# The context half of one attention block's first layer, run before and beside the experts of the block ahead of it

## The chip, the cores and the metric

One core of a Trainium2 chip runs the whole kernel. The metric is the device time of one execution in microseconds (us), the median of three runs.

## What is computed

Two blocks of two layers each work on 256 tokens of width 1024. Block 1 has a mixer and a mixture of 16 experts per layer; block 2 has attention and an MLP, on the tokens and, in layer 0, on 256 context tokens as well. All of it is float32.

```python
def first_block(x, c, ...):
    for layer in range(2):
        sh1, sc1, g1, sh2, sc2, g2 = split(silu(c) @ mod_w[layer] + mod_b[layer], 6)
        x = x + g1 * (even_mixer if layer == 0 else odd_mixer)(rms_norm(x) * (1 + sc1) + sh1)
        x = x + g2 * moe(rms_norm(x) * (1 + sc2) + sh2)      # 2 of 16 experts per token
    return x

def second_block(x, c, ctx, c_ctx, ...):
    xc = ctx
    for l in range(2):
        ...                                   # six modulation vectors for x, six for xc
        y, yc = _token_mixers(h, hc, ..., with_ctx_out=l == 0)
        x = _layer_norm(ALPHA * x + g1 * y)
        x = _layer_norm(ALPHA * x + g2 * _sq_relu_mlp(x * (1 + sc2) + sh2, w_fc1[l], w_fc2[l]))
        if l == 0:
            xc = _layer_norm(ALPHA * xc + g1c * yc)
            xc = _layer_norm(ALPHA * xc + g2c * _sq_relu_mlp(xc * (1 + sc2c) + sh2c, w_fc1[l], w_fc2[l]))
    return x
```

In `_token_mixers` the queries of the tokens see the keys of the tokens and of the context; the queries of the context see the context's keys alone. So nothing in the context half of layer 0 needs block 1.

## The kernel before

Activations stand transposed: `xT` and `cT` hold 8 tiles of 128 channels by 256 tokens, for the tokens and the context. A weight matrix is read in strips of 1024 x 128 (512 KB, one load on SP's queue, L321). `split_w` (L333, L325) makes of a strip a rounded part `wh` on ACT and a rest `wl` on VectorE, and `linear` (L345 to L347) multiplies in three matmuls per 128 channels, 24 for a strip; the moving operand is 256 columns wide for one half, 512 for both.

The phases follow each other: `ev` (layer 0's mixer), `moe0`, `od` (layer 1's mixer), `moe1`, then for each layer of block 2 `at` (attention) and `ml` (output, norm, MLP).

In a `moe` phase a router (L664 on) ranks the experts by the number of their tokens; `values_load` (L870) reads the 16 expert numbers into registers of SP. `PASSES` lists seven passes of one, one, two, two, two, four and four experts, which share the 128 columns of the array; `prep` gathers the tokens of the passes of a group in `GROUPS`, `up_` multiplies by w1 and w3, `down` by w2, `combine` adds the result to `xT`. Each expert has 12 loads of 512 KB, 192 in a phase, used as they are, in float32 (L917). While `deep` is set, loads go to 11 buffers named `raw` and to the 8 split buffers `wh` and `wl`.

In layer 0 of block 2 both halves go through each stage together: projections 512 columns wide (`lin`), `attend` for the tokens over 512 keys and for the context over 256, `out2`, and `mlp2` with 64 strips, of which 16 are read and multiplied once for each half.

The modulation vectors are 24 groups of eight steps (`mod_steps`, L365 on): a step loads 512 KB and multiplies it by the condition in small matmuls on PE (L396), or, where `onv` says so, by operations on VectorE (L388). They wait in `queue`; `fill(n)` issues the next n wherever it stands, `need` those up to a named group.

The instructions of each engine stand in an order that is fixed when the kernel is built, planned from the order of the program and the waits; each engine takes its own in that order.

Of the kernel before, what the change touches and what calls it, by code (L numbers as in the profile page):

```python
# [19 lines left out]
S = 256  # L20
# [3 lines left out]
GROUPS = [[0, 1], [2, 3], [4, 5, 6]]  # L24
# [177 lines left out]
def body(tc, A, out, co, po):  # L202
# [4 lines left out]
    with ExitStack() as ctx:  # L207
# [19 lines left out]
        def U(dt=F32, name="u", bufs=1, pool=None):  # L227
            return (pool or pools[-1][0]).tile([128, 512], dt, tag=name, bufs=bufs, name=name)

        def K1(name, bufs=2, pool=None):  # L230
            return (pool or pools[-1][0]).tile([128, S], F32, tag=name, bufs=bufs, name=name)

        class Act:


            def __init__(self, n, w=S, dt=F32, name="a", bufs=None, pool=None):
                self.w, self.per = w, 512 // w
# [65 lines left out]

        turn, more, XR, XH = [0, -1, -1], [], 5, 1

        deep = [None]

        def load(src, sh=None, w=1024):
            turn[1] += 1
            if deep[0]:  # L310
                pool, tag, n = deep[0][turn[1] % len(deep[0])]
                t = pool.tile([128, 1024], F32 if tag == "raw" else F32R, tag=tag, bufs=n, name=tag)
                t = t if tag == "raw" else t.bitcast(F32)
                d = SY.dma_start(out=t[:, :w] if sh is None else t[:, :w].rearrange("p (a b) -> p a b", a=sh), in_=src)
                return t, d.ins.name
# [5 lines left out]
            SY.dma_start(out=dst, in_=src)  # L321
# [119 lines left out]
        def colsum(src, nk, w=S):  # L441
# [10 lines left out]
            e = U(name="cs", bufs=2)  # L452
# [5 lines left out]
        def rstd_of(dst, o, n, ep=0):  # L458
# [5 lines left out]
            t = U(name="nr", bufs=2)[:, :w]  # L464
# [189 lines left out]
        landed = mybir.DependencyInfo(mybir.DependencyClass.Sync, mybir.DependencyReason.DATA)  # L654
# [14 lines left out]
        def router(xg, rs, sh):  # L669
# [26 lines left out]
            def rank(v, n):  # L696

                t = pools[-1][0].tile([128, n, 2, 4], F32, tag=f"rk{n}", bufs=2, name="rk")
# [34 lines left out]
            big = lambda: pools[-1][0].tile([128, 2, 16, 16], F32, tag="pm", bufs=2, name="pm")  # L733
# [44 lines left out]
        def wide3(n):  # L778
            sh = {"P": [128, 2, 384], "PT": [128, 3, S], "xg": [128, 8, 384]}[n]
            return pools[-1][0].tile(sh, F32 if n == "xg" else F32R, tag=n, bufs=2, name=n)  # L780
# [65 lines left out]
        def moe(l):  # L846
# [733 lines left out]
```

## Time and profile before

| | us |
|---|---|
| median of 3 runs (lowest, highest) | 1975.26 (1973.67, 1975.89) |
| the profiled execution | 1974.64 |
| its span, from the first to the last instruction | 1972.9 |
| busy: PE, VectorE (DVE), ACT, POOL | 1788.7, 1092.9, 736.1, 125.0 |

The profile's mean granted clock of TensorE is 0.962 of full speed, and 440.50 MB are moved, 223 GB/s over the span. A busy PE in the profile isn't a PE at its peak: matmuls are pipelined, and their ends are modelled. The rows that matter stand below, by view. "Idle before" is the time that an engine stood idle just before an instruction, with what ended it behind the arrow.

### The profile page before, as it was taken

What the parts mean: (1) busy time and instruction counts of PE and PEld (TensorE: products, weight loads), DVE (VectorE), ACT (ScalarE), POOL (GpSimd) and SP (SyncE); (2) the same over time, 40 slices, a digit from 0 to 9 for tenths busy, and PEclk for the clock granted to TensorE, in tenths of its full rate; (3) what the DMA queues carried; (4) which work ended last, traced back from release to release, by engine and by line L of the source; (5) the groups of instructions that cost most, each with busy time, mean ns of one, the idle gap of its engine ahead of it and who ended that gap; (6) DMA issues with size and microseconds to landing.
All of it is one profiled execution on the core that took longest, in us unless ns stands there. A gap on an engine that the chain in (4) does not pass through costs nothing. (4 is left out here: it accounts for less than half of the span.)

```text
span 1972.9 us, 29820 instructions
## 1 busy us (share of the span) xinstructions
PE 1788.7 (91%) x11134; PEld 1244.2 (63%) x11134; DVE 1092.9 (55%) x2270; ACT 736.1 (37%) x1459; POOL 125.0 (6%) x148
## 2 busy tenths in 40 slices
PE   6799999768799997688999999999999999989997
PEld 3567644212686442126665679888888786569996
DVE  4986502102775121028778567578855767666665
ACT  3345301000483010003667456232323656544443
POOL 0900000000020000001000001000000200010000
PEclk8999999989899998898999999999999999999998
DMA  9566699999765999995111366455644220245551
GB/s 373 186 248 225 248 420 369 420 419 398 289 224 207 419 377 419 420 413 174 53 33 33 127 227 196 161 174 190 187 139 139 93 95 22 68 152 187 183 181 44
DMA packets 122270, 440.50 MB, mean 223 GB/s; under 512 B 13568, under 2 KB 13696, under 8 KB 121856
## 3 DMA queue, kind: packets, MB, share of 16 engines
q1 hardware_dynamic: 122112, 438.46, 60.6%
q8 instruction: 92, 1.51, 0.3%
q14 instruction: 66, 0.54, 0.1%
HBM read 437.35 MB, written 1.05 MB: 222 GB/s over the span
## 5 line engine op out<-in xcount | busy, mean ns | idle before, releaser
L333 ACT CAST wh<-raw 128x1024 fp32r<-128x1024 f32 (+1 forms) x258 | 261.0, 1015 | 282.7 <-PE psL L347 243.2
L325 DVE TENSOR_TENSOR wl<-raw,wh 128x1024 fp32r<-128x1024 f32 (+1 forms) x258 | 309.8, 1203 | 81.1 <-ACT wh L333 80.8
L345 PE MATMUL psL<-h,wh 128*128 128x256 f32 (+1 forms) x800 | 258.6, 323 | 7.8 <-ACT h L341 7.7
L346 PE MATMUL psL<-h,wl 128*128 128x256 f32 (+1 forms) x800 | 257.7, 322 | 2.8 <-DVE wl L325 2.8
L347 PE MATMUL psL<-h,wh 128*128 128x256 f32 (+1 forms) x800 | 255.7, 320 | 0.1
L345 PE MATMUL psL<-gh,wh 128*128 128x256 f32 (+1 forms) x576 | 185.1, 322 | 0.0
L346 PE MATMUL psL<-gh,wl 128*128 128x256 f32 (+1 forms) x576 | 184.6, 321 | 0.0
L917 PE MATMUL psab<-raw,xg 128*32 128x512 f32 (+2 forms) x580 | 142.2, 671 | 34.6 <-DMA raw<-w 26.1
L345 PEld LDWEIGHTS psL<-h,wh 128*128 128x128 f32 x800 | 154.1, 193 | 24.9 <-ACT h L341 8.8
L346 PEld LDWEIGHTS psL<-h,wl 128*128 128x128 f32 x800 | 153.9, 193 | 18.7 <-issue 6.5
L347 PEld LDWEIGHTS psL<-h,wh 128*128 128x128 f32 x800 | 153.6, 192 | 12.7 <-issue 2.5
L933 DVE SCALAR_TENSOR_TENSOR sa<-sa,gs,psab 128x512 f32<-128x512 f32 x14 | 10.5, 748 | 257.8 <-PE psab L917 257.8
L347 PE MATMUL psL<-o,wh 128*128 128x256 f32 (+1 forms) x384 | 120.6, 314 | 0.4
L341 ACT CAST yh<-psY 128x512 fp32r<-128x512 f32 x28 | 16.0, 586 | 280.1 <-PE psY L917 280.1
L345 PEld LDWEIGHTS psL<-gh,wh 128*128 128x128 f32 x576 | 109.5, 190 | 14.5 <-issue 5.8
L346 PEld LDWEIGHTS psL<-gh,wl 128*128 128x128 f32 x576 | 109.6, 190 | 11.1 <-issue 3.7
L917 PEld LDWEIGHTS psab<-raw,xg 128*32 128x32 f32 (+2 forms) x580 | 39.4, 136 | 107.1 <-issue 81.4
L917 PE MATMUL psab<-wh,xg 128*32 128x512 f32 (+2 forms) x212 | 87.2, 722 | 11.9 <-DMA wl<-w 9.0
L917 PE MATMUL psY<-raw,at 128*32 128x512 f32 (+2 forms) x308 | 91.6, 626 | 5.6 <-DMA raw<-w 5.2
L347 PE MATMUL psL<-gl,wh 128*128 128x256 f32 (+1 forms) x288 | 91.9, 319 | 0.0
L917 PE MATMUL psab<-wl,xg 128*32 128x512 f32 (+2 forms) x232 | 80.9, 692 | 11.2 <-DMA raw<-w 5.8
L1085 DVE SCALAR_TENSOR_TENSOR xT<-psL,mod2T,xT 128x256 f32<-128x256 f32 x80 | 38.7, 484 | 90.5 <-PE psL L347 90.3
(459 smaller groups left out, 3622.1 us busy)
## 6 DMA issues: line engine op xcount, KB each, us to landing
raw<-w SPq DMA_DIRECT2D x222, 512.0 KB, 9.9
raw<-fc SPq DMA_DIRECT2D x144, 512.0 KB, 3.4
raw<-mod_w SPq DMA_DIRECT2D x96, 512.0 KB, 6.0
raw<-w_mod SPq DMA_DIRECT2D x96, 512.0 KB, 4.3
wh<-w SPq DMA_DIRECT2D x82, 512.0 KB, 9.9
wl<-w SPq DMA_DIRECT2D x80, 512.0 KB, 9.9
raw<-wo SPq DMA_DIRECT2D x24, 512.0 KB, 4.4
raw<-wi SPq DMA_DIRECT2D x18, 512.0 KB, 3.3
```

The lines of the kernel that those rows point to most:

```text
L325: eng.tensor_sub(o, a, hi)
L333: SC.copy(hi[:, :w], raw[:, :w])
L341: SC.copy(hi, src)
L345: T.matmul(o, lhsT=wh, rhs=xh, start=start, stop=False)
L346: T.matmul(o, lhsT=wl, rhs=xh, start=False, stop=False)
L347: T.matmul(o, lhsT=wh, rhs=xl, start=False, stop=stop)
L917: r = T.matmul(o[w * i:w * i + w, :], lhsT=x[:, w * i:w * i + w], rhs=loads[i][0][:, c:c + 512], start=first, stop=last)
L933: V.scalar_tensor_tensor(sa, sa, gs, ob, op0=OP.mult, op1=OP.mult)
L1085: V.scalar_tensor_tensor(src2[s][:, n, :], o[:, s * S:s * S + S], mod2T[l][:, g, s, n:n + 1], src2[s][:, n, :], op0=OP.mult, op1=OP.add)
```

## The change

A new phase `ac` after `ev` runs `mixer2` and `out2` of layer 0 for the context alone. It stores the context's keys, values and low-rank keys, and the MLP's modulated input, to memory (`left`); layer 0's attention for the tokens (`"x"`) loads the keys and values back. `context_mlp` makes a list of 32 strips' work for each expert phase (two quarters of the MLP's width: 16 strips of fc1, 16 of fc2); `tiles` calls `beside`, which issues the next of the list, on average twice in nine calls in a pass of two experts, and once a call in a pass of four. The rest of layer 0 of block 2 works on 256 columns, with the tokens' norms spread over the strips as layer 1 has them.

Along with it: `GROUPS` has four groups, each gathered just before its first pass; an expert's number is read when its first load is issued; `combine` follows each pass; `deep` goes, so that loads have the 11 `raw` buffers, since the split buffers serve the strips; the modulation queue has another order, steps hold their matmuls until two or four loads are there, and no step of the MLP stages uses VectorE; several buffers and PSUM banks shrink.

```diff
-GROUPS = [[0, 1], [2, 3], [4, 5, 6]]
+GROUPS = [[0], [1, 2], [3, 4], [5, 6]]
...
-            if deep[0]:
-                pool, tag, n = deep[0][turn[1] % len(deep[0])]
...
@@ mod_steps
-                    for c in range(4):
-                        T.matmul(o[32 * c:32 * c + 32, :256], lhsT=cols[0][:, k, :], rhs=r[:, c * 256:(c + 1) * 256],
-                                 start=k == 0, stop=k == 7)
+                    if k == 0:
+                        st["held"], st["n"] = [], 4 if more else 2
+                    st["held"].append((k, r, landing[0]))
+                    if len(st["held"]) == st["n"]:
+                        for kk, rr, _ in st["held"]:
+                            for c in range(4):
+                                i = T.matmul(o[32 * c:32 * c + 32, :256], lhsT=cols[0][:, kk, :],
+                                             rhs=rr[:, c * 256:(c + 1) * 256], start=kk == 0, stop=kk == 7)
...
@@ moe
-            ids = [nc.values_load(idi[0:1, r:r + 1], engines=[mybir.EngineType.SP], min_val=0, max_val=NE - 1)
-                   for r in range(NE)]
+            def expert(r):
+                if r not in known:
+                    known[r] = nc.values_load(idi[0:1, r:r + 1], engines=[mybir.EngineType.SP], min_val=0, max_val=NE - 1)
+                return bass.ds(known[r], 1)
...
+                share[0] += {1: 0, 2: 2, 4: 9}[len(loads)]
+                while share[0] >= 9:
+                    share[0] -= 9
+                    beside(1)
...
+            share, strips = [0], context_mlp((2 * l, 2 * l + 1))
+
+            def beside(n):
+                for _ in range(min(n, len(strips))):
+                    strips.pop(0)()
...
-                    if len(todo) == 2 or p == NP:
-                        combine(todo)
-                        todo = []
-                if groups and GROUPS[groups[0]][0] == p + 2:
+                    combine(todo)
+                    todo = []
+                if groups and GROUPS[groups[0]][0] == p + 1:
                     pr.update(prep(groups.pop(0)))
-            deep[0] = None
+            beside(len(strips))
...
@@ attend, mixer2
-            for s in range(nq):
-                k0 = 0 if s == 0 else 256
-                nk = 512 - k0
...
                         scores(i, qb * 128, o[:, :nk])
+                        fill(1)
...
+            own, keys = (S, S) if part == "c" else (S, 512) if part == "x" else (512, 512)
...
+            def kept(n, t):
+                if part == "c":
+                    SY.dma_start(out=left[n], in_=t)
+                elif part == "x":
+                    SY.dma_start(out=t, in_=left[n])
...
+                if part:
+                    fill(per, True)
                 return o
+            per = 2 if part == "c" else 1
...
@@ out2
+            def put_away(k):
+                t = K1("hm", 2, bp)
+                V.tensor_scalar(t, cT[:, k, :], mod2T[l][:, 4, 1, k:k + 1], mod2T[l][:, 3, 1, k:k + 1], op0=OP.mult, op1=OP.add)
+                SY.dma_start(out=left["h"][:, k * S:k * S + S], in_=t)
...
+        def context_mlp(quarters):
+            hh, hl = Act(8, S, F32R, "chh"), Act(8, S, F32R, "chl")
+            gh, gl = Act(8, S, F32R, "cgh"), Act(8, S, F32R, "cgl")
+            def back():
+                for j in range(2):
+                    r = load(left["h"][:, j * 1024:j * 1024 + 1024])
+                    for k in range(4):
+                        split(hh(4 * j + k), hl(4 * j + k), r[:, k * S:k * S + S])
+            def up1(q, n):
+                if q == quarters[0] and n == 0:
+                    back()
+                o = ps()
+                linear(A["fc1"][0, 8 * q + n], hh, hl, o[:, :S])
+                t = K1("ct", 1)
+                SC.activation(t, o[:, :S], AF.Relu)
+                V.tensor_mul(t, t, o[:, :S])
+                split(gh(n), gl(n), t)
+            def down1(q, n):
+                o = ps()
+                linear(A["fc2"][0, q, n], gh, gl, o[:, S:])
+                residual(0, 5, n, o, (1,))
+            return [lambda f=f, q=q, n=n: f(q, n) for q in quarters for f in (up1, down1) for n in range(8)]
...
@@ the order of phases
-                for l, g in [(0, g) for g in range(2, 6)] + [(1, g) for g in range(6)]:
-                    later(("a", l, g), mod1(l, g))
-                for l in range(2):
-                    for g in range(6):
-                        later(("b", l, g), mod2(l, g))
+                for v in ("a02 b00 b01 b02 b03 b04 a03 a04 a05 b05 a10 a11 a12 a13 a14 a15 b10 b11 b12 b13 b14 b15").split():
+                    v = (v[0], int(v[1]), int(v[2]))
+                    later(v, (mod1 if v[0] == "a" else mod2)(*v[1:]))
...
+            SY.dma_start(out=cT, in_=A["cT"])
+            with phase("ac") as ap:
+                UW[0] = S
+                banks.clear(); banks.update(L=2, X=1, S=2, T=1, O=1, M=1)
+                os_ = mixer2(0, ap, None, "c")
+                out2(0, *os_, ap, 1)
+                settle()
+                UW[0] = 512
             with phase("moe0"):
-                banks.clear(); banks.update(ab=3, T=1, Y=2, X=2)
+                banks.clear(); banks.update(ab=2, Y=2, X=2, L=2)
                 moe(0)
-            SY.dma_start(out=cT, in_=A["cT"])
```

## Rows read from the trace of the kernel before

**Rows 1.** The first part of the page: busy us, share of span.

```profile
span 1972.9 us, 29820 instructions
...
PE 1788.7 (91%) x11134; PEld 1244.2 (63%) x11134; DVE 1092.9 (55%) x2270; ACT 736.1 (37%) x1459; POOL 125.0 (6%) x148
```

**Rows 2.** Busy us by stage and engine; then PE clock, DMA share, GB/s.

```profile
237.00:488.00 251.00, 211.30 (x1006) 83.10 (x1005) 37.59 (x91) 18.57 (x34) 0.00 (x0) 0.95 1.00 406
...
887.00:1102.00 215.00, 203.28 (x985) 132.15 (x985) 169.47 (x445) 130.04 (x319) 17.57 (x20) 0.98 0.20 68
1102.00:1556.00 454.00, 450.16 (x2696) 372.65 (x2696) 308.02 (x494) 171.84 (x281) 16.02 (x12) 1.00 0.53 173
1556.00:1714.00 158.00, 149.36 (x906) 110.42 (x904) 117.05 (x288) 97.74 (x229) 12.19 (x20) 0.99 0.18 59
1714.00:1973.00 259.00, 238.28 (x1869) 219.96 (x1868) 155.66 (x235) 111.90 (x189) 9.73 (x12) 0.97 0.46 149
```

**Rows 3.** The same view in stretches of 25 us.

```profile
0.00:25.00 25.00, 13.49 (x118) 4.98 (x118) 8.61 (x58) 6.67 (x16) 0.20 (x4) 1.00 0.93 357
...
375.00:400.00 25.00, 13.54 (x86) 2.88 (x84) 0.00 (x0) 0.60 (x1) 0.00 (x0) 0.80 1.03 419
...
1325.00:1350.00 25.00, 25.00 (x112) 20.71 (x111) 24.50 (x38) 5.27 (x5) 0.00 (x0) 1.00 0.67 221
...
1850.00:1875.00 25.00, 25.00 (x210) 25.00 (x210) 16.05 (x22) 11.58 (x20) 0.00 (x0) 1.00 0.54 182
```

**Rows 4.** PE's instructions in order of time: start, us, what, idle before.

```profile
244.71 13.90 PE L917 MATMUL psab<-raw,xg 128*128 128x512 f32 x32
...
332.23 0.66 PE L936 MATMUL psT<-cst,sa 128*128 128x128 f32 x4 [0.91 <-DVE sa L933]
...
893.19 0.79 PE L345 MATMUL psS<-h,wh 128*128 128x512 f32 x1 [5.75 <-ACT h L341]
...
1738.95 0.64 PE L396 MATMUL psM<-raw,cond2r 128*32 128x256 f32 x8
1739.52 0.38 PE L345 MATMUL psL<-o,wh 128*128 128x256 f32 x1
...
1957.97 0.28 PE L347 MATMUL psL<-o,wh 128*128 128x256 f32 x1
```

**Rows 5.** DMA issues: line, queue, count, size, median us to landing.

```profile
raw<-fc SPq DMA_DIRECT2D x144, 512.0 KB, 3.4
```

**Rows 6.** Busy time by stage, the attention of layers 0 and 1 alone.

```profile
953.00:1102.00 149.00, 146.28 (x705) 88.03 (x704) 114.43 (x353) 100.73 (x266) 8.77 (x12) 1.00 0.09 29
...
1612.00:1714.00 102.00, 97.46 (x536) 63.12 (x535) 74.81 (x208) 64.02 (x156) 5.63 (x12) 1.00 0.13 42
```

**Rows 7.** Instructions by line and shape: busy us, mean ns, idle before.

```profile
L325 DVE TENSOR_TENSOR wl<-raw,wh 128x1024 fp32r<-128x1024 f32 x240 | 297.8, 1242 | 79.7 <-ACT wh L333 79.4
L333 ACT CAST wh<-raw 128x1024 fp32r<-128x1024 f32 x240 | 250.2, 1045 | 277.4 <-PE psL L347 240.4 <-DMA raw<-ev_in 13.4 <-DMA raw<-fc 9.3
...
L388 DVE SCALAR_TENSOR_TENSOR sq<-raw,cond,sq 128x512 f32<-128x512 f32 x112 | 77.4, 746 | 1.0 <-DMA raw<-w_mod 1.0
...
L1219 DVE TENSOR_REDUCE nm<-psS 128x1 f32<-128x512 f32 x64 | 44.0, 687 | 13.4 <-PE psS L1434 8.2 <-PE psS L347 4.7
...
L1488 DVE TENSOR_TENSOR t<-t,psL 128x256 f32<-128x256 f32 x48 | 20.2, 420 | 21.1 <-ACT t L1487 21.0
...
L341 ACT CAST gh<-t 128x256 fp32r<-128x256 f32 x48 | 19.5, 406 | 1.4 <-DVE t L1488 1.4
...
L1487 ACT ACTIVATE t<-psL 128x256 f32<-128x256 f32 x48 | 18.4, 383 | 51.1 <-PE psL L347 51.1
...
L1219 DVE TENSOR_REDUCE nm<-psS 128x1 f32<-128x256 f32 x32 | 13.2, 418 | 5.7 <-PE psS L347 3.7 <-PE psS L1434 1.9
```

**Rows 8.** One line's instructions, the expert list as integers: first and last start.

```profile
L745 DVE CAST idi<-ids x2: 166/166/167, 227.0 to 622.3; 128x16 int32<-128x16 f32 x2
```

**Rows 9.** SP's queue in order of time: start, us, transfers issued.

```profile
205.23 11.40 SPq L321 DMA_DIRECT2D raw<-mod_w  x13
236.73 5.28 SPq L314 DMA_DIRECT2D raw<-w  x9
```

More of the change, by code (lines that the diff above doesn't have):

```diff
@@ L320, in load @@
             dst = t[:, :w] if sh is None else t[:, :w].rearrange("p (a b) -> p a b", a=sh)
-            SY.dma_start(out=dst, in_=src)
+            landing[0] = SY.dma_start(out=dst, in_=src).ins.name
             return t
@@ L943, in down @@
                 for k in range(4):
-                    ls = [load(A["w2"][l][bass.ds(ids[r], 1), k * 128:(k + 1) * 128, :].rearrange("o p n -> p (o n)"))
+                    ls = [(load(A["w2"][l][expert(r), k * 128:(k + 1) * 128, :].rearrange("o p n -> p (o n)")), landing[0])
                           for r in PASSES[p]]
@@ L1268, in lin @@
                 segs = [(0, m)]
-                if m == 512 and l:
+                if m == 512:
                     segs = [(0, S), (S, m)]
-                elif m == 512 and n in first:
-                    segs = [(S, m), (0, S)]
-                linear(A["wi2"][l, n] if w is None else w, hh, hl, o, 0 if l == 0 else 0, segs=segs)
-                if free and l == 0:
-                    fill(1, True)
+                linear(A["wi2"][l, n] if w is None else w, hh, hl, o, segs=segs)
+                if part:
+                    fill(per, True)
                 return o
+            per = 2 if part == "c" else 1
             o_ab = [[U(F32R, "o", 8, bp) for _ in range(4)] for _ in range(2)]
@@ L1281, in values @@
             def values():
-                vab = [U(name="vab", bufs=2).rearrange("p (a b) -> p a b", b=256) for _ in range(2)]
+                vab = [U(name="vab", bufs=keys // 256, w=512).rearrange("p (a b) -> p a b", b=256) for _ in range(keys // 256)]
                 w = [split_w(load(A["vi2"][l, u], 4)) for u in range(2)]
-                for m in range(4):
+                for m in range(own // 128):
                     if free:
@@ L1295, in values, with chunk @@
                     SC.copy(vab[m // 2][:, m % 2, :], o)
-                if free and l == 0:
-                    fill(1, True)
+                kept("va", vab[-1].rearrange("p a b -> p (a b)"))
+                if part:
+                    fill(per, True)
                 return vab
-            def chunk(i, n, gname=None):
+            def chunk(i, n, gname=None, key=None):
                 o = lin(i, n)
@@ L1306, in chunk @@
                     head_norm(t, t, gname, n)
-                rope(t, 64)
+                if part != "c":
+                    rope(t, 64)
+                if key and part:
+                    kept(key, t[:, keys - S:keys])
+                    n = keys
                 hl = [U(F32R, "qk", 12) for _ in range(2)]
@@ L1393, in mixer2 @@
             kvh, kvl = split_w(load(A["ukv2"][l]))
-            vc = [U(name="h", bufs=16, pool=bp) for _ in range(4)]
+            vc = [U(name="vc" if part == "c" else "h", bufs=2 if part == "c" else 16, pool=bp, w=512) for _ in range(keys // 128)]
             o_c = [[U(F32R, "h", 16, bp) for _ in range(4)] for _ in range(2)]
-            for m in range(4):
+            for m in range(keys // 128):
                 o = ps()
@@ L1468, in mlp2 @@
         def mlp2(l, hh, hl, bp):
-            nq = 2 if l == 0 else 1
-            spare = lambda: l == 0 and len(queue) > (8 if q else 44) and fill(1)
-            each, both = [(s,) for s in range(nq)], [tuple(range(nq))]
+            spare = lambda: l == 0 and len(queue) > (8 if q else 32) and fill(1)
+            if l == 0:
+                whole_norm(0, "ln2", 1)
             for q in range(4):
-                if l == 0 and q == 1:
-                    settle()
-                    onv.extend([1] * 7)
```

222 lines of the change are left out of this document (109 added, 113 removed).

## The prediction, made before the changed kernel was built

> **What bounds the kernel now.** I read four views in this order: the first part of the page, the busy time per stage, the instructions grouped by line and shape, and the order of work on PE and on SP. The page says 91% busy TensorE over a span of 1972.9 us [rows 1]; read alone, that leaves nothing to gain by moving work about. The stages say otherwise [rows 2]. In the expert stage of layer 0 (237 to 488, 251 us; layer 1's, 637 to 887, is its like) the DMA share is 1.00 at 406 GB/s: the weights set the pace, 192 loads of 512 KB. In one stretch of the four-expert passes PE is busy for 13.54 of 25 us at 419 GB/s [rows 3]; a load takes 0.524 MB / 419 GB/s = 1.25 us. In block 2 it is the reverse: the MLP stage of layer 0 has PE busy for 450 of 454 us and the DMA at 0.53. So PE time is free in one place and short in another, and the change moves it there. What counts is how much of it is really free.
>
> **PE's price list.** A 256-column matmul of a linear costs 25/210 = 0.119 us, a 512-column one 25/112 = 0.223 us [rows 3]. A strip (24 matmuls) is 2.86 us for one half and 5.35 us for both. An expert's float32 matmul is two instructions: 32 of them, 16 matmuls, stand in 13.90 us [rows 4], so an up stage of any pass is 13.9 us, a down stage 6.9 us, and seven passes 146 us.
>
> **Removed: the context half from block 2, layer 0.** The two stages of layer 0 take 669 us (887 to 1556) [rows 2]. What stays, the token half, is what layer 1 does today from 1556 to its last matmul of fc2 at 1957.97 [rows 4], 402 us, less the context keys it projects itself (four strips and 48 matmuls of the values: 4 x 2.86 + 48 x 0.119 = 17 us) and less its eight modulation steps at 0.57 us (from the start of one, x8 at 1738.95, to the linear that follows at 1739.52, both [rows 4]), 5 us. That gives 380 us, and, as an estimate, 3 us for the context's last norm: 383. Saved: 286 us. Layer 1 itself loses those eight steps: 5 us. The reloaded keys and values are five small transfers on SP that need no result, so they can lie beside the projections; a late one would cost about the landing time of an uncrowded queue, 3.4 us [rows 5]. I take nothing and keep 5 x 3.4 = 17 us for the bound.
>
> **Added: the context attention ahead of the experts.** PE work: 10 strips and 48 value matmuls, 34 us; eight strips of the output, 23 us; the small products of the third attention (q, k and v from the low ranks), 7 us. Attention: today eight calls with both halves take 149 us, with the token half alone 102 us [rows 6]; the difference, 47 us, is the least for the context half. Standing alone its chain is exposed: the maximum over 256 keys takes 418 ns against 687 over 512 [rows 7], and 102 x 0.61 = 62 us. Then 64 modulation steps come into this phase that the old order ran in the two MLP stages of block 2, 32 of them on VectorE (112 operations, 77.4 us [rows 7], hidden behind PE there): 64 x 0.57 = 36 us on PE. The chain without them: 5 us until PE has a modulated strip (5.75 at the start of today's attention, where POOL does half of the splits, as it will here [rows 4]); 27 for six projections and the values (23 of PE, but 22 loads with the steps' own); 70 for the attention with the low-rank strips, 8 of it beyond the 62; 26 for the output strips; 10, an estimate, for the norm. Together 138 us, in which PE, with 34 + 23 + 7 + 30 of its own (the attention's products, half of what 512 keys take), has some 44 us of gaps. If all steps fit the gaps the phase takes 138 us; if none, 174. Its 89 loads are 111 us, below both. The stores of keys and values stand on SP and wait for results; every load behind one waits too, up to 3.4 + 1.05 + 1.24 = 5.7 us [rows 5, 7] for each of five, 28 us. Router work on other data may start in the tail. I take **150 us**, bounds 130 and 195.
>
> **Added: 32 MLP strips in each expert stage.** Per stage 34 loads more (two bring the stored activations back): 34 x 1.25 = 42.5 us if the DMA stays the bound. On PE it is 32 x 2.86 = 92 us, beside 146 us of experts and some 40 us of gathering, transposes and combining: 277 us against 226 x 1.25 = 283 us of loads. Nearly equal sums don't overlap fully, so I go by passes, with the new code's 11 load buffers (the old one lent the idle split buffers too: 19). Passes 0 and 1 have no strips, and PE takes about 50 us against 30 us of loads; only 11 loads can run ahead. Passes 2 to 4: per pass 13.9 + 6.9, 2.67 strips (7.6), gathering (half of 32 x 0.119 and transposes, 3), combining (3), the wait for Silu's product and the transposes (0.91 + 0.66 [rows 4]): 36 us, 108 in all against 100 us of loads. Passes 5 and 6: a step is four loads and a strip's, 6.25 us, with 1.7 + 2.86 us of PE: bound by loads, 150 us less the 11 that ran ahead, 14 us, and the last combining 4. Sum: 50 + 108 + 136 + 4, and 8, an estimate, for the edges between the passes = 306 us.
>
> The start moves forward. Today the router's expert list is ready at 227.0 [rows 8], but SP reads all 16 entries before the first expert load goes out at 236.73, and the load before it was among 13 begun at 205.23 and done issuing at 216.6 [rows 9]. The new code reads an entry when it needs it: first load about 228.5. 228.5 + 2 (landing) + 306 = 536, against 488 now: **+48 us per stage**. Bounds: below, loads alone, 42.5 - 8.5 and a few us for earlier starts, +25; above, the strips' own chain in passes 5 and 6: cast 1.05, subtract 1.24, 2.86 of matmuls, Relu 0.38, product 0.42, cast 0.41 [rows 7] and the tile's 0.86 make 7.2 us a step where each waits for the one before, against 6.25; 24 x 0.95 = 23 us, +75 with the edges. Strips wait on ACT and VectorE behind Silu and the splits; both are little used there (18.57 and 37.59 of 251 us [rows 2]). The combining after every pass instead of two adds VectorE operations only; the same matmuls.
>
> The extra loads are priced at the rate of the four-expert stretch. The Trainium skill speaks against that (DMA: Bandwidth & Descriptors, section Where 436 GB/s comes from): for HBM to SBUF the HBM side, about 358 GB/s, should bind. The stretch shows 419, so the rule doesn't hold in this stage; by it the 68 loads would cost 68 x 0.21 = 14 us more.
>
> **Steps that cost nothing.** Holding four modulation steps until all their loads are in leaves matmuls and loads as they were, and PE waits once instead of four times; it is covered by the linears around it. One bank less for the experts' first products: Silu has read both before the next pass begins, beside the down stage (6.9 us).
>
> **Sum.** 1972.9 - 286 - 5 + 150 + 2 x 48 = 1928 us of span. The profiled execution took 1974.64 us for a span of 1972.9, so 1929.6; the median of the three runs is 0.6 above it: 1930 us, 45 us or 2.3% faster. About 0.2%, 4 us, is what a measurement of this kernel can tell from no change.
>
> **Rivals.**
> - *The strips hide entirely.* The expert stages stay bound by loads from end to end, +25 each: 1930 - 46 = 1884. For it: the DMA at 1.00 today; against it: today's 19 buffers make that so. Chance 0.2.
> - *The strips are not hidden* (slower). In the PE queue a strip stands between two groups of expert tiles; while it runs, 11 buffers fill and loads stop. If its 92 us add to the stage (251 - 8.5 + 92 = 334, +83), the time is 1930 + 70 = 2000. It decides from +70 per stage, (291 - 150) / 2. For it: passes 0 to 4 have more PE work than loads in the new order; against: passes 5 and 6, where 24 of 32 strips lie, have 6.25 us of loads per 4.6 of PE. Chance 0.15.
> - *The attention phase is a chain*: stores hold the loads back and modulation steps find no gaps, 195 us: 1975, no change. For it: SP is in order; against: SP runs ahead of need today, as its 13 loads in 11.40 us show [rows 9]. Chance 0.1.
> - *The extra loads come slower*: at the 357 GB/s of the kernel's first 25 us [rows 3], 1.47 us each: 68 x 0.22 = 15 us, 1945. The rule of the Trainium skill named above (DMA: Bandwidth & Descriptors, Where 436 GB/s comes from) would come to the same. Against it: 419 in the stage itself. Chance 0.05.
> - *Forecast*: 0.5.
>
> **How the numbers follow.** 1930 is the likeliest. The range 1870 to 1990 takes in the first, third and fourth rivals and most of the bounds (all at their lower ends: 1850; all upper: 2029), and leaves out the slower one. Faster: 0.5 + 0.2 + 0.05 and four tenths of the third = 0.79; same 0.05; slower 0.16.
>
> **What the new profile should show.** A phase of 140 to 165 us between the first mixer and the router with PE some 85% busy; the first expert load within 2 us of the expert list; expert stages of 300 us or so from first load to last tile, DMA share about 0.95 and PE busier; DMA bytes up by some 36 MB (62 weight loads of 0.524 MB, and the activations stored and reloaded); layer 0 of block 2 in about 383 us, with matmuls of 256 columns alone and no VectorE accumulation. I am wrong if an expert stage is over 325 us, if the context phase is over 195, or if PE waits for the reloaded keys.

## The result and the profile after

The changed kernel takes 2037.38 us (median of four runs, 2031.79 to 2041.77) against 1974.47 us before: 3.2% slower, ratio 1.0317, 95% interval 1.029 to 1.0345. The forecast was 1930 us, the range 1870 to 1990; the time lies outside it, on the other side of no change.

The first part of the page of the changed kernel, and its bytes (the profiled execution took 2041.77 us, the slowest of the four, so the differences of spans below come to some 4 us more than those of the medians):

```profile
span 2040.0 us, 33843 instructions
...
PE 1850.7 (91%) x12848; PEld 1366.3 (67%) x12848; DVE 1134.5 (56%) x2367; ACT 820.6 (40%) x1633; POOL 122.5 (6%) x160
...
HBM read 473.00 MB, written 2.88 MB: 233 GB/s over the span
```

PE's share is the same 91% as in [rows 1], with 62 us more of busy time. The stages show where. Busy time by stage of the changed kernel (columns as in [rows 2]); the stages are the context's attention, the router, layer 0's experts, layer 1's mixer and router, layer 1's experts, the tokens' attention and MLP in layer 0, and layer 1 of block 2:

```profile
204.00:382.00 178.00, 166.61 (x1442) 116.85 (x1444) 93.28 (x262) 90.05 (x234) 8.65 (x16) 0.99 0.78 279
382.00:413.00 31.00, 23.17 (x175) 11.16 (x167) 15.78 (x56) 9.74 (x21) 1.59 (x2) 0.67 0.37 132
413.00:756.00 343.00, 315.24 (x1846) 186.71 (x1846) 119.84 (x241) 69.76 (x111) 0.00 (x0) 0.98 0.92 358
756.00:884.00 128.00, 113.81 (x1009) 95.29 (x1009) 85.38 (x182) 74.17 (x149) 16.35 (x18) 0.93 0.67 241
884.00:1233.00 349.00, 319.23 (x1882) 189.24 (x1882) 121.44 (x248) 70.42 (x112) 0.00 (x0) 0.98 0.90 351
1233.00:1395.00 162.00, 147.08 (x820) 103.88 (x821) 125.31 (x305) 89.64 (x210) 9.98 (x16) 0.95 0.31 96
1395.00:1631.00 236.00, 227.41 (x1748) 210.54 (x1748) 154.53 (x241) 117.06 (x205) 11.08 (x12) 0.98 0.51 155
1631.00:2040.00 409.00, 376.56 (x2664) 325.63 (x2662) 267.76 (x510) 206.10 (x408) 21.80 (x32) 0.97 0.33 104
```

Both expert stages have PE busy for some 92% of the time and the DMA below 1.00: the bound has moved. With the stages cut at marks that both traces have (the expert list as integers, the last combining of a stage, the first matmul of layer 1 of block 2):

| | before, us | after, us | difference | forecast |
|---|---|---|---|---|
| start to expert list, layer 0 | 227.0 | 412.2 | +185.2 | +150 |
| list to last combining, layer 0 | 266.8 | 344.0 | +77.2 | +48 |
| to the list of layer 1 | 128.5 | 128.2 | -0.3 | 0 |
| list to last combining, layer 1 | 266.1 | 348.8 | +82.7 | +48 |
| layer 0 of block 2 | 675.8 | 406.4 | -269.4 | -286 |
| layer 1 of block 2 | 408.7 | 400.4 | -8.3 | -5 |
| span | 1972.9 | 2040.0 | +67.1 | -45 |

112 us are missing: 35 in the context phase and the router, 29 and 35 in the expert stages, 17 in the tokens' half of layer 0 of block 2; its layer 1 gave 3 more than forecast.

### The profile page after: what moved, and what is told of

Its sections match the earlier page's. It is cut to its first block, busy times and chain, and to the rows that moved or that the text cites. A ratio compares the mean times of both kernels' runs of the same rounds, so it can differ in the third digit from the quotient of the medians.

```text
span 2040.0 us, 33843 instructions
## 1 busy us (share of the span) xinstructions
PE 1850.7 (91%) x12848; PEld 1366.3 (67%) x12848; DVE 1134.5 (56%) x2367; ACT 820.6 (40%) x1633; POOL 122.5 (6%) x160
## 2 busy tenths in 40 slices
DMA packets 134529, 478.25 MB, mean 234 GB/s; under 512 B 14929, under 2 KB 17105, under 8 KB 134097
## 5 line engine op out<-in xcount | busy, mean ns | idle before, releaser
L323 DVE TENSOR_TENSOR wl<-raw,wh 128x1024 fp32r<-128x1024 f32 (+1 forms) x321 | 386.0, 1205 | 142.2 <-ACT wh L331 141.5
L343 PE MATMUL psL<-h,wh 128*128 128x256 f32 x792 | 231.6, 293 | 9.7 <-ACT h L339 8.1
L344 PE MATMUL psL<-h,wl 128*128 128x256 f32 x792 | 230.0, 291 | 2.2 <-DVE wl L323 2.2
L345 PE MATMUL psL<-h,wh 128*128 128x256 f32 x792 | 228.7, 290 | 0.0
L343 PE MATMUL psL<-gh,wh 128*128 128x256 f32 x512 | 146.6, 287 | 0.8 <-ACT gh L339 0.8
L344 PE MATMUL psL<-gh,wl 128*128 128x256 f32 x512 | 145.9, 286 | 0.0
L345 PE MATMUL psL<-o,wh 128*128 128x256 f32 x352 | 101.1, 287 | 1.6 <-DVE o L323 1.1
L344 PE MATMUL psL<-cgh,wl 128*128 128x256 f32 x256 | 76.8, 300 | 16.1 <-DVE wl L323 16.1
L344 PE MATMUL psL<-chh,wl 128*128 128x256 f32 x256 | 74.3, 290 | 13.8 <-DVE wl L323 13.8
L343 PE MATMUL psL<-hh,wh 128*128 128x256 f32 x256 | 77.2, 302 | 6.2 <-ACT hh L511 3.2
L343 PE MATMUL psL<-chh,wh 128*128 128x256 f32 x256 | 75.6, 295 | 6.6 <-ACT wh L331 6.5
```

What stands on the lines that cost most here:

```text
L323: eng.tensor_sub(o, a, hi)
L343: T.matmul(o, lhsT=wh, rhs=xh, start=start, stop=False)
L344: T.matmul(o, lhsT=wl, rhs=xh, start=False, stop=False)
L345: T.matmul(o, lhsT=wh, rhs=xl, start=False, stop=stop)
```

## The experiments

"Stage" is layer 0's expert stage, from the expert list to the last combining (in the run with strips at the end, to the last strip).

**What the strips cost, and what the rest of the new stage costs.**

```diff
-            share, strips = [0], context_mlp((2 * l, 2 * l + 1))
+            share, strips = [0], []
```

> Left out of the computation: the MLP of the context in layer 0 of block 2 (all 64 strips and the reload of its input). The changed kernel's expert stages took 341 and 347 us from the first load to the end, 86 us more than before from the expert list on, counting the 9 us earlier start. Theory A, the strips cost nearly all of their time on TensorE (32 x 2.86 = 92 us), and the rest of the new stage costs nothing: 250 to 258 us per stage, and about 2037 - 2 x 87 = 1863 us. Theory B, the strips cost little beyond their loads (34 x 1.25 = 43 us, up to 50), and the other 36 us come from the 11 load buffers in place of 19, the later gathering and the combining after every pass: 290 to 300 us per stage, and about 1940 us.

```diff
-            deep[0] = [(wp, "raw", RAW)] * RAW + [(more[0], "raw", XR)] * XR + \
-                [(q, t, n) for q, n in ((wp, HL), (more[0], XH)) for t in ("wh", "wl") for _ in range(n)]
+            deep[0] = [(wp, "raw", RAW)] * RAW + [(more[0], "raw", XR)] * XR
```

> The kernel before, with 11 load buffers in the expert stages in place of 19. Theory A: within 5 us per stage, so 1975 to 1985 us. Theory B: 20 to 35 us per stage, so 2015 to 2045 us, with the DMA share well under 1.00 in the passes of one and two experts.

```diff
-                share[0] += {1: 0, 2: 2, 4: 9}[len(loads)]
+                share[0] += 0
```

> The changed kernel, with all 32 strips of a stage behind the last pass of its experts instead of among the passes. Theory A, the strips are hardly hidden among the passes: no more than 10 us per stage above the changed kernel, 2037 to 2060 us. Theory B, about 45 us of each stage's 92 are hidden by the experts' loads: 35 to 45 us more per stage, 2105 to 2130 us.

Without strips 1916.43 us (one run), stage 282.5; the kernel before with 11 buffers 1993.8 us (one run), stage 275.1; strips at the end 2120.38 us (one run), stage 392.5. The first two lie between the theories, the third is theory B's. Together they give a split, if the parts add, which wasn't tested. The strips cost 344.0 - 282.5 = 61.5 us of the stage. The 11 buffers cost 275.1 - 266.8 = 8.3 us. What else changed in the stage, above all gathering in four groups and combining after every pass, is left with 282.5 - 275.1 = 7.4 us; no run takes that apart. Two later runs whose edits lie outside this stage have it at 345.7 and 346.3 us, so each part is good to some 2 us. Behind the experts the strips cost 110 us; among them 48.5 us less. So a good part is hidden, but not enough. The two halves of the stage, cut where the product of the fifth pass is transposed, in the kernel before:

```profile
227.00:357.00 130.00, 124.90 (x533) 60.97 (x534) 29.07 (x95) 13.64 (x27) 0.00 (x0) 0.97 0.91 363
357.00:494.00 137.00, 98.08 (x535) 30.16 (x533) 19.36 (x38) 9.06 (x13) 0.00 (x0) 0.90 1.01 411
```

the same without strips:

```profile
408.00:542.00 134.00, 126.86 (x512) 63.32 (x513) 32.65 (x99) 11.18 (x21) 0.00 (x0) 0.95 0.86 330
542.00:690.00 148.00, 106.12 (x568) 35.08 (x566) 24.49 (x52) 10.98 (x17) 0.00 (x0) 0.90 1.00 408
```

and in the changed kernel:

```profile
412.00:563.00 151.00, 147.16 (x660) 78.96 (x660) 48.61 (x129) 24.57 (x47) 0.00 (x0) 0.96 0.88 331
563.00:756.00 193.00, 168.08 (x1187) 107.75 (x1186) 72.23 (x115) 45.20 (x64) 0.00 (x0) 0.99 0.95 377
```

The DMA share of 1.00 in [rows 2] was a mean over two halves. In the first, PE is busy for 124.9 of 130 us; in the second, the DMA for all of it. The first half had no room for strips: 6 of the 32 stand there (144 of their 768 matmuls), and each costs 2.8 us (151 - 134 = 17), nearly its whole 2.86 us on PE. The other 26 cost 1.7 us each (193 - 148 = 45).

**The late reading of the expert numbers, alone.**

```diff
-            ids = [nc.values_load(idi[0:1, r:r + 1], engines=[mybir.EngineType.SP], min_val=0, max_val=NE - 1)
-                   for r in range(NE)]
+            known = {}
+
+            def expert(r):
+                if r not in known:
+                    known[r] = nc.values_load(idi[0:1, r:r + 1], engines=[mybir.EngineType.SP], min_val=0, max_val=NE - 1)
+                return bass.ds(known[r], 1)
...
```

> The kernel before, with one part of the change alone: an expert's number is read when its first load is issued, not all 16 first. Forecast: the first expert load stands 1 us behind the list of experts instead of 9.7 and 9.4 us, both stages end 8.5 us sooner, and the time falls by 17 us to 1957. Rival, the stage's end is set by TensorE or by something that does not start sooner (gathering the tokens of the first passes): no more than 4 us per stage, 1967 or above.

1976.73 us, ratio 1.0013 (1.0003 to 1.0024): the rival. The first load does go out sooner, at 227.00 instead of 236.73 us, yet the stage ends 266.5 us behind the list. The same stretches of that kernel:

```profile
260.00:275.00 15.00, 15.00 (x40) 6.82 (x39) 1.44 (x2) 0.60 (x1) 0.00 (x0) 1.00 0.99 379
275.00:300.00 25.00, 25.00 (x95) 9.31 (x94) 2.82 (x4) 1.77 (x3) 0.00 (x0) 1.00 0.93 352
300.00:335.00 35.00, 33.87 (x169) 17.44 (x169) 9.42 (x22) 4.80 (x10) 0.00 (x0) 1.00 0.85 324
```

and of the kernel before:

```profile
260.00:275.00 15.00, 15.00 (x41) 6.84 (x40) 1.44 (x2) 0.60 (x1) 0.00 (x0) 1.00 1.02 419
275.00:300.00 25.00, 25.00 (x98) 9.53 (x97) 3.52 (x5) 1.77 (x3) 0.00 (x0) 1.00 1.03 419
300.00:335.00 35.00, 34.09 (x164) 17.34 (x164) 9.42 (x22) 4.80 (x10) 0.00 (x0) 1.00 0.92 350
```

PE is full in both. It doesn't idle ahead of the first load either: in the kernel before, it gathers the tokens of two groups first, and the first expert tile starts 17.7 us behind the list (244.71, [rows 4]); with the late reading it starts 11.2 us behind, and the second group's gathering stands behind it. The earlier loads fill the buffers, and then the DMA runs below its rate: by these rows it moves 3.2 MB less up to 335 us, 7.6 us of loading at 419 GB/s. So of the 10 us won at the start 2 are left there, and at the stage's end, counted from the list, 0.3.

**The order of the passes.**

```diff
-PASSES = [[0], [1], [2, 3], [4, 5], [6, 7], [8, 9, 10, 11], [12, 13, 14, 15]]
-CAPS = [128 // len(p) for p in PASSES for _ in p]
+PASSES = [[0], [8, 9, 10, 11], [2, 3], [4, 5], [6, 7], [1], [12, 13, 14, 15]]
+CAPS = [128] * 2 + [64] * 6 + [32] * 8
```

> The kernel before, with the same seven passes in another order: a pass of four experts stands second, a pass of one sixth, so that passes bound by loads alternate with passes bound by TensorE. The stretches of the kernel before show TensorE busy for 85 of 85 us from 240 to 300 and 34 of 35 to 335 (passes of one and two experts), and the DMA at 1.03 with TensorE idle for a third of the time from 360 to 450 (passes of four). Theory, each half of the stage has its own bound and the order decides how much the two overlap: from 267 us after the expert list to some 255, 10 to 12 us per stage, so about 1951 us. Rival, the stage is bound by its 192 loads from end to end (DMA share 1.00): no change, 1970 to 1979 us.

> The same order, and an expert's number read when its first load is issued. Alone that reading gave nothing (1976.73 us), which the theory of two bounds puts down to the TensorE-bound first passes. If so, with a four-expert pass second the earlier start counts: 6 to 8 us per stage more, so about 1937 us. Rival, reading the numbers one by one costs SP what the earlier start gives: the same time as with the order alone, within 4 us.

```diff
-PASSES = [[0], [1], [2, 3], [4, 5], [6, 7], [8, 9, 10, 11], [12, 13, 14, 15]]
+PASSES = [[8, 9, 10, 11], [0], [2, 3], [4, 5], [6, 7], [1], [12, 13, 14, 15]]
...
```

> The kernel before with numbers read late, as in the run of 1952.67 us, but a four-expert pass first and the first one-expert pass second. Theory of two bounds: the loads are the bound from the first tile on; 0 to 4 us per stage better, 1945 to 1953 us. Rival, the first pass now waits for four loads per step and for more gathering work on VectorE, and the time is lost: 1956 us or above.

The order alone: 1965.25 us, ratio 0.9954 (0.9937 to 0.997), stage 262.1. With the numbers read late: 1952.67 us, 0.9888 (0.9872 to 0.9905), stage 254.3. With a four-expert pass first: 1951.46 us, the same ratio and interval, stage 254.3. The direction is the theory's; for the order alone the size is less than half of it (4.7 us of the stage against 10 to 12; the kernel before has PE busy for 60 of 60 us from 240 to 300, where the expectation has 85 of 85). The late reading, worth nothing before, is now worth the expected 8 us per stage. These two runs beat the kernel before by 22 us or 1.1%, without moving any context work. Stretches of the last one:

```profile
260.00:300.00 40.00, 32.05 (x146) 10.34 (x138) 2.88 (x4) 0.60 (x1) 0.00 (x0) 0.89 1.03 419
300.00:335.00 35.00, 30.70 (x117) 10.65 (x116) 5.59 (x10) 2.94 (x5) 0.00 (x0) 1.00 1.03 419
335.00:360.00 25.00, 25.00 (x129) 13.37 (x128) 5.20 (x15) 3.63 (x8) 0.00 (x0) 1.00 1.03 419
```

From 260 to 450 us every stretch has the DMA at 1.03 and 418 to 420 GB/s, and PE idles in most of them: there the loads are now the bound.

**The same order in the changed kernel.**

```diff
-                share[0] += {1: 0, 2: 2, 4: 9}[len(loads)]
+                share[0] += {1: 0, 2: 0, 4: 12}[len(loads)]
```

(with the first new order of passes)

> The changed kernel in the same order of passes, with all 32 strips in the passes of four experts (four in three steps) and none in those of two. By the marks of the run without strips, the 8 strips in passes of two cost 16 us per stage (TensorE is the bound there) and the 24 in passes of four 1.7 us each. Theory of two bounds: 8 strips at 1.7 save 3 us, the order 10 us more: 10 to 15 us per stage, 2008 to 2018 us. Rival, the strips' own chain (cast, subtract, matmuls, Relu, product) sets their cost wherever they stand, and packing them denser makes it worse: 2037 us or above.

2043.06 us, ratio 1.0356 (1.0333 to 1.0378), stage 348.3: the rival's number. In the changed kernel the order and the denser strips together give nothing. Whether the order alone would give something there, and the packing takes it away, no run shows. A stretch of PE's instructions in order of time, in the changed kernel as it is (start, us, idle before), shows a step of a four-expert pass:

```profile
651.36 1.92 PE L928 MATMUL psab<-raw,xg 128*32 128x512 f32 x16
653.75 0.38 PE L343 MATMUL psL<-chh,wh 128*128 128x256 f32 x1 [0.46 <-ACT wh L331]
655.01 0.38 PE L344 MATMUL psL<-chh,wl 128*128 128x256 f32 x1 [0.88 <-DVE wl L323]
...
657.91 1.92 PE L928 MATMUL psab<-raw,xg 128*32 128x512 f32 x16
```

The step is 6.55 us: four experts' tiles, a wait for the strip's cast, a wait for its subtraction, its matmuls. Five loads at 1.25 us are 6.25 us. Loads (6.25), the step with its waits for the strip's chain (6.55) and PE's own work (1.9 + 2.9, and the passes' other work between the steps) stand close together. The next three runs try to take them apart.

**Loads, chain, matmuls.**

The first edit gives each strip a constant tile of zeros in place of its load:

```diff
-            wh, wl = split_w(load(src, nk, nk * 128), pool, nk * 128)
+            wh, wl = split_w(load(src, nk, nk * 128) if raw is None else raw, pool, nk * 128)
...
-                linear(A["fc1"][0, 8 * q + n], hh, hl, o[:, :S])
+                linear(None, hh, hl, o[:, :S], raw=ctile["iota"][0][:, 528:1552])
...
-                linear(A["fc2"][0, q, n], gh, gl, o[:, S:])
+                linear(None, gh, gl, o[:, S:], raw=ctile["iota"][0][:, 528:1552])
```

> Left out of the computation: the loads of the context's 64 strips (a constant tile stands in for each; cast, subtract, matmuls and the rest stay). Theory of loads, the strips in the four-expert passes cost their transfers there: a step of four experts and a strip falls from 6.06 to 6.55 us to some 5.0 us, and the stage from 344 us after the expert list to 305 to 312; about 1968 us. Rival, the strips' own chain sets the step (Relu of one strip stands ahead of the cast of the next on ACT: TensorE waits 0.46 us for the cast and 0.88 us for the subtraction in each step): the step stays above 6 us, the stage above 330, and the time above 2010 us.

The second issues load, cast and subtraction one strip ahead:

```diff
+            def ahead():
+                for _ in range(2 - len(split_ahead)):
+                    if todo_w:
+                        split_ahead.append(split_w(load(todo_w.pop(0), 8)))
+                return split_ahead.pop(0)
...
-                linear(A["fc1"][0, 8 * q + n], hh, hl, o[:, :S])
+                linear(None, hh, hl, o[:, :S], w=ahead())
...
-                linear(A["fc2"][0, q, n], gh, gl, o[:, S:])
+                linear(None, gh, gl, o[:, S:], w=ahead())
```

> The changed kernel, with each strip's load, cast and subtraction issued one strip ahead of its matmuls, so that TensorE finds them done. Theory of loads: no more than 4 us per stage, 2029 us or above. Rival, the strips' chain: TensorE's 18 us of waits for cast and subtraction per stage go, and most of the time with them, 10 to 18 us per stage, 2001 to 2017 us.

The third edit leaves 8 of the 24 matmuls of a strip; `third` is set for the strips alone:

```diff
-                    mm3(og, wh[:, c], wl[:, c], xh(k, *ag), xl(k, *ag), k == 0, k == nk - 1)
+                    if third:
+                        T.matmul(og, lhsT=wl[:, c], rhs=xh(k, *ag), start=k == 0, stop=k == nk - 1)
+                    else:
+                        mm3(og, wh[:, c], wl[:, c], xh(k, *ag), xl(k, *ag), k == 0, k == nk - 1)
```

> Left out of the computation: 16 of the 24 matmuls of each context strip in the expert stages (those with the rounded weights); loads, casts, subtractions, the wait for the subtraction and the rest stay. 32 x 16 x 0.119 = 61 us of matmuls go from each stage. Theory, TensorE's time is the bound beside the loads (315 busy of 342 us): the stage falls to what the loads leave, from 344 us after the expert list to 305 to 320, and the time to 1960 to 1990 us. Rival, the strips' chain through ACT and VectorE is the bound: no more than 12 us per stage (matmuls are part of that chain, but the loads stand 0.3 us below it), 2013 us or above.

Without the strips' loads 2019.4 us (one run), stage 335.6: the rival's side. With a third of their matmuls 2014.99 us (one run), stage 325.1, layer 1's 325.3: between the two expectations by the stages, which fall by 19 and 24 us. Only 27 of these 42 us are left in its span (2013.2 us): the stages that the edit doesn't touch are 16 us longer in its trace, at a granted clock of 0.90 to 0.95 in places where the changed kernel had 0.93 to 0.97, so its total says less than its stages. Each edit takes away 8 to 24 us of a stage, where no strips at all take 61.5. The halves without the strips' loads, then with a third of the matmuls:

```profile
405.00:557.00 152.00, 149.80 (x680) 81.41 (x681) 48.08 (x129) 23.66 (x47) 0.00 (x0) 0.95 0.85 313
557.00:741.00 184.00, 173.65 (x1169) 104.33 (x1167) 66.69 (x111) 40.20 (x59) 0.00 (x0) 1.00 0.85 317
```

```profile
411.00:556.00 145.00, 134.41 (x558) 67.54 (x558) 48.26 (x129) 24.74 (x47) 0.00 (x0) 0.96 0.87 336
556.00:736.00 180.00, 132.55 (x776) 61.53 (x776) 71.27 (x115) 45.34 (x63) 0.00 (x0) 0.94 1.00 407
```

With the strips' loads gone PE is busy for 173.65 of 184 us; with most of their matmuls gone the DMA is at 1.00 over 180. So the second half takes 184 us without the one, 180 without the other, 193 with both and 148 without the strips. Neither theory of a single bound is right: taking one away uncovers the other some 10 us below. What the chain adds on its own stays open: both edits shorten it too.

The split issued one strip ahead was meant to remove the chain, and cost 40 us: 2077.47 us, ratio 1.0525 (1.0507 to 1.0543), stage 364.6, outside both expectations. What SP waited for there, two rows (us in total, times, longest):

```profile
SPq L319 <- PE psab L928: 126.3, 64, 11.8
SPq L319 <- PE psY L928: 65.5, 38, 6.0
```

In the changed kernel the first row is 128.6 us in 62 waits and the second 46.8 us in 38; waits for a strip's subtraction (DVE wl) are 7.8 us in 4 up to the stage's end, against 6.1 in 3. A possible reading, not shown, is that a strip loaded early holds one of 11 buffers while the experts' loads wait; PE's waits for cast and subtraction stayed (19.5 us against 19.2). The experiment didn't remove what it was to remove, so it says nothing on the chain.

**The modulation steps in the context phase.**

```diff
+                if thin and 0 < k < 7:
+                    return
...
-                        st["held"], st["n"] = [], 4 if more else 2
+                        st["held"], st["n"] = [], 1 if thin else 4 if more else 2
```

> Left out of the computation: in the context's attention phase, six of the eight steps of each modulation group (loads and matmuls), so 47 or 48 of 63 or 64 steps. Theory, the phase is bound by TensorE (busy 166.6 of 178 us) and every step costs its time there, 0.57 us: 27 us less, about 2010 us. Rival, the phase is bound by the attention's chain or by the stores on SP, and the steps lie in gaps: no more than 8 us less, 2029 us or above.

`thin` holds during the context phase; the steps that are left don't wait for each other's loads. The whole time (3135.21 us, one run) can't be used: with other modulations the router sends more tokens to an expert than fit, and the overflow branch runs. The phase itself lies ahead of that. Its last output matmul in the changed kernel, and in this one:

```profile
357.69 0.28 PE L345 MATMUL psL<-h,wh 128*128 128x256 f32 x1
```

```profile
326.54 0.28 PE L345 MATMUL psL<-h,wh 128*128 128x256 f32 x1
```

It stands 31 us earlier, but 4 of these lie ahead of the phase: its first projection starts at 204.22 us in the changed kernel and at 200.38 in this one. From there to the row shown 153.5 us become 126.2, 27.3 us for some 45 steps (470 of their matmul instructions there against 112, eight to a step), 0.61 each: the theory of TensorE, expected at 27 us. The edit takes the steps' loads away too, but these aren't the bound; the phase up to that matmul, changed kernel, then this run:

```profile
204.00:358.00 154.00, 152.52 (x1258) 109.56 (x1260) 82.67 (x232) 76.91 (x199) 8.65 (x16) 1.00 0.76 274
```

```profile
204.00:327.00 123.00, 122.56 (x873) 96.03 (x876) 78.30 (x229) 72.65 (x194) 7.83 (x15) 1.00 0.48 156
```

PE is full in both, with the DMA at 0.76 and 0.48. The steps lie in no gaps.

**Two parts undone: the store's buffers, the steps on VectorE.**

```diff
-                if part == "x":
-                    onv.append(1)
...
-                t = K1("hm", 2, bp)
+                t = K1("ho", 8, bp)
```

> Two parts of the changed kernel undone, which lie in stages of their own. (1) The context's stored activation gets 8 buffers in place of 2: VectorE waited 4.2 and 2.8 us there for a store to leave, with the router's work behind it on VectorE and ACT. Theory, the tail of the context phase is a chain through these buffers: from the last output strip's matmul to the expert list 54.5 us becomes 45 to 48. Rival, the context's norm and the modulation steps set the end: 54 as it is. (2) In layer 0's attention for the tokens the eight modulation steps that ran on VectorE (32 operations, 23 us, in the first 60 us, where VectorE is busy for 53.9 us) run on TensorE (8 x 0.57 = 4.6 us). Theory, the first projections are bound by VectorE now that half of the work they hid behind is gone: from the stage's first matmul to the end of attention 158 us becomes 146 to 150. Rival, the attention's own chain is the bound: 158 to 163. Together 15 to 19 us by the theories (2018 to 2022 us), none by the rivals.

2017.06 us, ratio 1.0218 (1.0201 to 1.0235): 20 us less, both theories. (1) What was waited for in the tail of the context phase of the changed kernel (us in total, times, longest):

```profile
ACT cs L460 <- DMA left_h<-hm: 9.6, 1, 9.6
...
DVE hm L1485 <- DMA left_h<-hm: 6.9, 2, 4.2
```

The first row is the router's own sum on ACT, behind the context's stores. With 8 buffers both are gone, and the list follows the last output matmul by 46.9 us instead of 54.5. How much of that is the buffers' is less sure: in eight traces with two buffers, the changed kernel's and those of other runs, this tail is 48.4 to 54.6 us, so they are worth 1.4 to 7.6 us. (2) In the tokens' attention, its first 60 us in the changed kernel, and what VectorE's largest group was:

```profile
1236.00:1296.00 60.00, 53.40 (x313) 43.63 (x314) 53.90 (x116) 30.83 (x69) 4.19 (x4) 0.89 0.54 169
```

```profile
L386 DVE SCALAR_TENSOR_TENSOR p<-raw,cond,p 128x512 f32<-128x512 f32 x28 | 20.7, 777 | 0.0
```

With these steps on PE, the same stretch:

```profile
1226.00:1286.00 60.00, 59.50 (x414) 49.99 (x415) 42.89 (x106) 37.83 (x88) 2.94 (x4) 0.94 0.58 196
```

From the first projection to the first output strip 146.4 us become 133.4, 13 us less where 8 to 12 were expected (there up to the end of attention). In the eight traces with these steps on VectorE the stretch is 145.3 to 150.8 us, so this part is clear.

## Why the prediction was wrong

**Right.** TensorE's price list and the saving in block 2 by direction; the first expert load 1.2 and 1.0 us behind the list; layer 0's list and load in these two rows:

```profile
412.19 0.17 DVE L751 CAST idi<-ids 128x16 int32<-128x16 f32 x1
```

```profile
413.43 35.99 SPq L319 DMA_DIRECT2D raw<-w  x22
```

The bytes came out as told, 478.25 MB against 440.50. PE waited for no reloaded key. Of the three signs of being wrong that the prediction named, one came: an expert stage of over 325 us. The extra loads came at 419 GB/s where nothing else bound (the run with a third of the matmuls has 1.03 and 419 GB/s from 620 to 680 us), so the rival of slower loads fell, and the rule of the Trainium skill (DMA: Bandwidth & Descriptors, Where 436 GB/s comes from; about 358 GB/s) disagrees with the trace after the change as it did before.

**The expert stages, 64 us.** The forecast of +48 comes to 56.5 for the strips with all that goes along and 8.5 off for the earlier start. The strips alone measured 61.5, near enough: a third of their 92 us of matmuls is hidden, as foreseen. What failed stands around them:
- The start 8.5 us earlier: the load was earlier, the gain 0.3 us, because PE is full in the first passes and used the wait for gathering. The forecast's own sum had PE at 50 us against 30 us of loads there, and still took the earlier load for an earlier end.
- "Only 11 loads can run ahead" was said, and its price not taken: 8.3 us.
- "The combining after every pass instead of two adds VectorE operations only", and the fourth group costed at nothing: 7.4 us are left for the two and whatever else changed. The matmuls of the combining are as many as before (112 instructions in the trace); those of the gathering are 128 in the stage instead of 96, over the same columns in all.

61.5 + 8.3 + 7.4 - 0 = 77.2. The root is one reading: "the weights set the pace" from a mean DMA share of 1.00, where [rows 2] also had PE at 211.30 of 251 us. "Some 40 us of gathering, transposes and combining" beside 146 us of experts made 186 of that; 211 + 92 = 303 us would have been the larger sum, above the 283 of loads (PE's busy time is an upper bound there, as the last section shows). Of the rivals, "not hidden" named the outcome (+70 decides; it came to +77 and +83) and half of the mechanism: the strips' 92 us were not added whole, the buffers were a part.

**The context phase and router, 35 us.** The chain without steps was put at 128 us to the last output matmul. 153.5 us measured, less some 59 steps at 0.61 in that stretch, 36 us, is 118. So the chain is shorter than thought, and "some 44 us of gaps" for the steps don't exist: they cost 36 us, not 12. That is 14 of the 35. The other 21 are the tail: 54.5 us against 10 for the norm and 24 for the router as it was (the mixer's last output matmul at 203.3 to the list at 227.0). 7.6 of them by the two traces compared are the two-buffer store; in other traces with two buffers the tail is up to 6 us shorter, so it may be 1.4, and the rest this one execution's. The mechanism is another than foreseen: the forecast had stores hold up SP's loads, and here VectorE waited, with the router's work queued behind it there and on ACT. The remaining 13 (46.9 with 8 buffers, less 34), the context's norm and the steps ahead of the router, were not taken apart and stay open. The rival of the chain (195 us, chance 0.1) came near the 185 measured: it was right that the steps find no gaps, and not that the loads are held back.

**The tokens' half, 17 us.** The template was layer 1's stage of today, which has no steps on VectorE. In layer 0 one group of eight stands there, hidden until now by projections of both halves. That cover went with the context: 13 us. So did another: layer 1's first projection, which stands first here in the kernel before and then in the changed one, now waits 7.36 us for the norm between the layers, and did not wait before.

```profile
1564.22 0.47 PE L345 MATMUL psS<-h,wh 128*128 128x256 f32 x1
```

```profile
1639.59 0.58 PE L343 MATMUL psS<-h,wh 128*128 128x256 f32 x1 [7.36 <-ACT h L339]
```

13 and 7 are more than the 17, because the template was cut too early: at 1556 us layer 0 of the kernel before still had matmuls of fc2 to do, up to 1562. Counted from 1564.22 the prediction's own rule gives 677 - 375 = 302 us saved and not 286, so that 33 us fell short, and some 13 of them were not taken apart.

**Where the loss lies.** By the price list the strips took 48 x 2.49 + 16 x 2.86 = 165 us out of block 2. In the expert stages they cost 61.5 and 67.5 us (348.8 against 281.3 without them in layer 1), and the buffers 8 each: 146. That part of the move pays a little, even with the 7.4 us per stage that are left over. The other 104 us saved in layer 0 of block 2 are those of the attention and of the moved modulation steps, and the phase that took both in costs 185.

The range was also added up wrong: the prediction's own lower bounds give 1930 - 20 - 46 = 1864 us and not 1850, and its upper ones 2046 and not 2029 with the 17 us that it kept for reloaded keys. Nothing above hangs on that.

## What to carry to other kernels

A busy share of 1.00 over a stage says nothing of its parts: cut the stage where its work changes kind, and put work only into the part whose other engine idles, counted from that engine's measured busy time and not from a sum of its known instructions. Before moving work beside a bound stage, try to make the stage have one bound (here by the order of its passes, 1.1% with an earlier first load that alone is worth nothing). And work that is removed was also cover: look for what was hidden behind it.

## What the runs showed that was not expected

Some of PE's work behind a wait for loads ran at half the clock. Without strips, a four-expert tile step (16 instructions) takes 3.48 and 3.61 us after waits of 4.95 and 3.16 us, and 1.93 us after 1.42 us. The length of the last wait doesn't tell it alone: further on, a step takes 3.64 us after 1.74 us, and another 1.92 us after 2.97. The rows in order of time:

```profile
572.24 3.48 PE L928 MATMUL psab<-raw,xg 128*32 128x512 f32 x16 [4.95 <-DMA raw<-w]
577.14 1.93 PE L928 MATMUL psab<-raw,xg 128*32 128x512 f32 x16 [1.42 <-DMA raw<-w]
582.23 3.61 PE L928 MATMUL psab<-raw,xg 128*32 128x512 f32 x16 [3.16 <-DMA raw<-w]
```

The windows of the first two (PE clock third from the end):

```profile
572.30:575.60 3.30, 3.30 (x16) 0.60 (x16) 0.00 (x0) 0.00 (x0) 0.00 (x0) 0.52 1.02 418
577.20:579.00 1.80, 1.80 (x16) 0.36 (x16) 0.00 (x0) 0.00 (x0) 0.00 (x0) 1.00 1.05 430
```

The granted clock was 0.52 and 1.00, about the levels of 1.2 and 2.4 GHz. So a PE that waits for loads shows more busy time than the same work takes when it is fed, and a busy share in a load-bound stretch is an upper bound of what PE needs.
